# A hybrid decoder step: the prompt's last 16 tokens take gathered expert rows, and dense expert values come out with features in partitions

## The chip, the cores and the metric

The kernel runs on one core of one Trainium2 chip. The metric is the device time of one execution in microseconds (us), start to end. The program is written in a tile language whose scheduler sets the order of the instructions of each engine when the kernel is built; on the chip each engine then works through its own list in that order.

## The reference, cut to what matters

Two layers, each with a mixer (four kinds of heads side by side), a cross-attention and an expert part. 256 prompt tokens and 8 sample tokens go through them together, 264 columns in all. The change concerns the expert part. For every token and each of 8 heads it picks 16 of 16384 experts from 128 x 128 keys; an expert is a row of `u` and a row of `v`, 1024 numbers each:

```python
top_s, pick = lax.top_k(cand, PEER_TOPK)
e = jnp.take_along_axis(cidx, pick, axis=-1)
g = jax.nn.softmax(top_s, axis=-1)
act = jax.nn.gelu(jnp.einsum('td,thkd->thk', hb, u_tab[e]).astype(jnp.float32))
return jnp.einsum('thk,thkd->td', (g * act).astype(hb.dtype), v_tab[e])
```

So a token needs 128 rows of u, a gelu, a weight for each, and the weighted sum of 128 rows of v.

## The kernel before, in words

**Two ways to do the experts.** The 256 prompt tokens are done densely: all 16384 rows of u are multiplied with all 256 tokens, and a token's weight is zero for an expert that it did not pick. The 8 sample tokens are done sparsely: their 128 rows are gathered by index. The function is `peer`, from line 1585 on.

**Dense u** (`u_tile`, line 1638). Experts come in 128 tiles of 128. A tile of u (128x1024, 512 KB) is loaded by SP into one of three buffers `w`, split into a high part `wh` (ScalarE, line 313) and a low part `wl` (VectorE, line 298), and multiplied with the normed tokens, split likewise into `hh` and `hl` (`proj`, line 342): 8 pieces of the features times 3 products are 24 matmuls of 256 columns, called mm in the trace. ScalarE takes the gelu into HG0 (first 64 tiles) or HG1. `mm`, the helper, records every matmul at line 288. In the order's rows, names after the arrow are the two operands.

**Choosing and gating.** While the first 64 tiles run, VectorE and TensorE choose the experts of the prompt in two halves of 128 tokens, then of the sample tokens (lines 1651 to 1702). Then 64 gating steps (loop over `t4`, line 1745) make for 4 tokens each a 128x128 matrix of weights out of two one-hot matrices `ga` and `gb` (8 f16 matmuls into g), multiply it into HG, and compute one more tile of u.

**Sample rows.** In every fourth gating step one sample token gets its turn: for the first 32 steps `sample_u` (line 1708), then `sample_v`. `sample_u` gathers 128 rows of u (`us`, by the index tile `gi`) through GpSimd's queue into one of the three `w` buffers, SP broadcasts the token (`hd`, in DRAM) into `hb`, one buffer of 128x1024, and VectorE multiplies and sums them in one instruction (line 307) into `ac` (`sac`); three small instructions make its column of `wz`. `sample_v` gathers the rows of v and adds them up by 4 narrow matmuls, called sv, into `os_`.

**Dense values** (loop over `i2`, line 1773). A tile of v is loaded and split as u is, and HG is split into `ghl`. The output has tokens in partitions: 4 accumulators `acc` (pv in the trace) of 128 tokens x 512 features, 12 matmuls of 512 columns a tile. At the end `total` (line 1801) copies each accumulator, transposes it in four matmuls, adds it to the residual `x`, which has features in partitions, and squares it for the next norm.

**What sets the order.** The scheduler, from its own estimates of when an instruction can start. Hand-set places are the sv matmuls (kept together, given priority) and the last pv matmuls with the transposes.

Of the kernel before, what the change touches and what calls it, by code (L numbers as in the profile page):

```python
# [230 lines left out]
NF = 4  # L231
XT = 12
GS = 16384.0
# [10 lines left out]
def emit(tc, A, O, layers=(0, 1)):  # L244
# [305 lines left out]
    def rwkv(l, bp_, mp, cm, vc, inp, pre, st_rs, ymix):  # L550
# [85 lines left out]
        def unit(c, n0, zz=None):  # L636
# [69 lines left out]
            for i in range(1, 6):  # L706
# [3 lines left out]
                xl = tl([128], "xl", "xl")  # L710
# [874 lines left out]
    def peer(l, vc, xo, oo, xe, following):  # L1585
# [23 lines left out]
        hd = pe.enter_context(tc.tile_pool(name="d%d" % l, bufs=1, space=MemoryType.DRAM)).tile([8, 1024], F32, name="hd")  # L1609
        gi = fp.tile([128, 2, 8], I32, name="gi")  # L1610
        gs = fp.tile([128, 8], F32, name="gs")
# [5 lines left out]
        for c in range(16):  # L1617
            if c == 4:
                rms(tp, vc('norm_ffn'), r, hf, (hh, hl))
                for j in range(2):  # L1620
                    o = ps([8, 512], "h8")
                    for k in range(4):
                        T.transpose(o[:, k * 128:k * 128 + 128], hf[:, 4 * j + k, 256:264], ident)
                    h8 = tp.tile([8, 512], F32, name="h8", tag="sk")
                    S.copy(h8, o)
                    nc.sync.dma_start(hd[:, j * 512:j * 512 + 512], h8)
# [7 lines left out]
        HG0 = h0p.tile([128, 64, 256], F32, name="HG0")  # L1634
# [3 lines left out]
        def u_tile(i2, t0=0):  # L1638


            o = proj(A['ud'][l, i2], (hh[:, :, 0:256], hl[:, :, 0:256]), 256)
            d = HG0[:, i2, :] if i2 < 64 else HG1[:, i2 - 64, :]
            if t0:
                a = fp.tile([128, 256], F32, name="ua", bufs=2)
                act(a[:, 0:t0], o[:, 0:t0], AF.Gelu_apprx_tanh)
                tt(d[:, 0:t0], d[:, 0:t0], a[:, 0:t0], OP.mult)
            if t0 < 256:
                act(d[:, t0:256], o[:, t0:256], AF.Gelu_apprx_tanh)

        cur_tag[0] = "ps"  # L1650
        for i in range(2):
# [22 lines left out]
            tt(el[:, 1, ti], wt[:, 0, ti], wt[:, 1, ti], OP.subtract)  # L1674

# [25 lines left out]
        ts(gi, o[:, 0:2, :], float(l * 16384), op0=OP.add)  # L1701
        V.tensor_copy(gs, o[:, 2, :])
# [17 lines left out]
        def sample_v(b):  # L1720
            v = wp.tile([128, 1024], F32, name="w", tag="w", bufs=3)
            nc.gpsimd.indirect_dma_start(out=v, out_offset=None, in_=A['vd'].rearrange("l a b d -> (l a b) d"),
                                         in_offset=bass.IndirectOffsetOnAxis(ap=gi[:, 1, b:b + 1], axis=0))

            with together():
                for j in range(4):
                    mm(os_[j * 32:j * 32 + 32], wz[:, b, :], v[:, j * 256:j * 256 + 256], start=b == 0, stop=b == 7, skip=True)

        def sample_out():
# [5 lines left out]
            d = x[:, :, 256:264].rearrange("p (j c) b -> p c j b", c=2)  # L1735
            tt(d, d, o.rearrange("p c (j q) -> p c j q", j=4)[:, :, :, 0:8], OP.add)
# [4 lines left out]
            [128, 64, 256], F32, name="HG1")  # L1741
        ac = fp.tile([128, 4, 8], F32, name="sac")
        wz = fp.tile([128, 8, 32], F32, name="wz")
        os_ = ps([128, 256], "sv", "pr")
        for t4 in range(64):
# [124 lines left out]
```

## Time and profile before

| | |
|---|---|
| median of 3 runs | 2450.73 us (2449.32 to 2453.59) |
| profiled execution | 2446.82 us |
| its span, first to last instruction | 2445.1 us |
| TensorE busy | 2374.8 us, 97% |
| VectorE busy | 1749.7 us, 72% |
| ScalarE busy | 1378.9 us, 56% |
| moved by DMA | 480.63 MB |

The profile is one execution. Busy time is a union: two overlapping instructions of one engine count once. Matmuls overlap, so a matmul's own length says little of what it costs; the distance between two starts does. In layer 0 the choosing of experts runs from about 447 to 603 us, the gating to 852, the values from 858 to 1220; in layer 1 the expert part ends with the kernel. "PEclk" is the granted clock of TensorE as a share of 2.4 GHz.

### The profile page before, as it was taken

The page shows a single profiled execution, that of the slowest core. Times are in us where ns is not written, and L with a number is a line of the kernel's source. Part 1 is how long each engine was busy: PE and PEld are TensorE (multiplying, and loading weights), DVE is VectorE, ACT ScalarE, POOL GpSimd, SP SyncE. Part 2 cuts the span into 40 slices and gives each one's busy share as a digit, 9 for nine tenths or more (in the row PEclk, how much of TensorE's full clock was granted, in tenths as well). Part 3 has the DMA queues.
Part 4 walks back from the last instruction along what each step waited for, and adds up shares of the span by engine and source line. Part 5 has one row for each costly group of instructions (what it writes and reads, how often), then busy time and mean ns, then how long its engine had stood idle before and what let it go on. Part 6 is the DMA issues. An engine that isn't in the chain of part 4 may idle for free.

```text
span 2445.1 us, 46669 instructions
## 1 busy us (share of the span) xinstructions
PE 2374.8 (97%) x17292; PEld 2123.9 (87%) x17292; DVE 1749.7 (72%) x3875; ACT 1378.9 (56%) x2826; POOL 267.6 (11%) x288
## 2 busy tenths in 40 slices
PE   9898999999999999999998989999999999999998
PEld 7776979999999988878787779899999999888886
DVE  6757767997698855565568567689967987555555
ACT  5445565554687744544554456655547876444444
POOL 5741000000000000000057400000000000000000
PEclk9999999999999999999999999999999999999999
DMA  8733775555675555565577428755556755566554
GB/s 286 231 110 113 268 300 201 174 179 174 205 235 186 191 178 189 193 208 187 188 230 226 125 95 311 273 191 174 178 181 214 232 182 184 185 189 188 187 188 137
DMA packets 146372, 480.63 MB, mean 197 GB/s; under 512 B 20288, under 2 KB 37728, under 8 KB 141024
## 3 DMA queue, kind: packets, MB, share of 16 engines
q1 hardware_dynamic: 129088, 423.46, 52.8%
q0 software_dynamic: 17056, 54.17, 7.4%
q8 instruction: 137, 2.24, 0.4%
q14 instruction: 91, 0.75, 0.1%
HBM read 468.53 MB, written 9.03 MB: 195 GB/s over the span
## 4 chain that ended last, share of the span: by engine, by line
PE 88%; DMA 5%; ACT 2%; DVE 2%; issue 1%; SPq 1%; POOL 1%; DVEq 0%; ACTq 0%; POOLq 0%
PE mm L288 43%; PE pv L288 29%; PE g L288 3%; PE mv L288 2%; DMA kvp<-in_kc 2%; PE asc L288 1%; PE mk L288 1%; DMA kvp<-in_vc,vidx 1%; PE xo L288 1%; PE xm L288 1%; PE sc L288 1%; PE xl L288 1%; PE xp L288 1%; PE apv L288 1%; DVE wl L298 1%
## 5 line engine op out<-in xcount | busy, mean ns | idle before, releaser
L313 ACT CAST wh<-w 128x1024 fp32r<-128x1024 f32 x662 | 694.3, 1050 | 756.8 <-PE pv L288 358.4
L298 DVE TENSOR_TENSOR wl<-w,wh 128x1024 fp32r<-128x1024 f32 x662 | 807.3, 1221 | 432.5 <-ACT wh L313 427.8
L288 PE MATMUL mm<-hh,wh 128*128 128x256 f32 (+1 forms) x2176 | 545.9, 288 | 3.7 <-ACT HG L310 2.9
L288 PE MATMUL mm<-hl,wh 128*128 128x256 f32 (+1 forms) x2176 | 536.2, 284 | 0.0
L288 PE MATMUL pv<-wh,ghl 128*128 128x512 f32 x2048 | 524.5, 396 | 0.4 <-ACT ghl L313 0.4
L288 PEld LDWEIGHTS pv<-wh,ghl 128*128 128x128 f32 x2048 | 385.1, 188 | 92.8 <-ACT ghl L313 0.9
L288 PEld LDWEIGHTS mm<-hh,wh 128*128 128x128 f32 x2176 | 410.3, 189 | 5.6 <-ACT HG L310 4.0
L288 PEld LDWEIGHTS mm<-hl,wh 128*128 128x128 f32 x2176 | 410.2, 189 | 3.3 <-issue 3.3
L288 PE MATMUL mm<-hh,wl 128*128 128x256 f32 (+1 forms) x2176 | 300.5, 281 | 0.0
L288 PE MATMUL pv<-wl,ghl 128*128 128x512 f32 x1024 | 283.6, 396 | 0.0
L288 PEld LDWEIGHTS mm<-hh,wl 128*128 128x128 f32 x2176 | 276.3, 188 | 0.4 <-issue 0.4
L288 PEld LDWEIGHTS pv<-wl,ghl 128*128 128x128 f32 x1024 | 192.4, 188 | 46.5 <-DVE wl L298 0.8
L310 ACT ACTIVATE gb<-ga,ewt 128x128 f16<-128x128 f16 x512 | 173.1, 433 | 19.8 <-DVE ga L298 16.2
L1226 POOL DMA_INDIRECT kvp<-in_kc,pidx x128 | 144.9, 1132 | 234.6 <-ACT eh L310 179.0
L288 PE MATMUL mm<-eh,wh 128*128 128x264 f32 x624 | 162.0, 294 | 0.0
L288 PE MATMUL mm<-el,wh 128*128 128x264 f32 x624 | 160.5, 290 | 0.0
L288 PEld LDWEIGHTS mm<-eh,wh 128*128 128x128 f32 x624 | 117.9, 189 | 4.9 <-issue 3.7
L288 PEld LDWEIGHTS mm<-el,wh 128*128 128x128 f32 x624 | 118.1, 189 | 3.0 <-issue 2.1
L298 DVE TENSOR_TENSOR ghl<-HG,ghl 128x256 fp32r<-128x256 f32 x256 | 106.7, 417 | 0.0
L313 ACT CAST ghl<-HG 128x256 fp32r<-128x256 f32 x256 | 101.8, 398 | 2.4 <-DVE HG L298 2.4
L298 DVE TENSOR_TENSOR HG<-HG,g 128x256 f32<-128x256 f32 (+31 forms) x254 | 86.2, 347 | 16.7 <-PE g L288 15.9
L1710 POOL DMA_INDIRECT w<-in_us,gi x16 | 16.8, 1053 | 713.3 <-DVE wl L298 418.9
(674 smaller groups left out, 3304.6 us busy)
## 6 DMA issues: line engine op xcount, KB each, us to landing
w<-in_ud SPq DMA_DIRECT2D x256, 512.0 KB
w<-in_vd SPq DMA_DIRECT2D x256, 512.0 KB
w<-in_w_in SPq DMA_DIRECT2D x46, 512.0 KB
kvp<-in_kc SPq DMA_DIRECT2D x128, 128.0 KB
xkt<-in_mk SPq DMA_DIRECT2D x16, 1024.0 KB
xkt<-in_mv SPq DMA_DIRECT2D x16, 1024.0 KB
w<-in_peer_wq SPq DMA_DIRECT2D x32, 512.0 KB
w<-in_x_wk SPq DMA_DIRECT2D x16, 512.0 KB
```

The costliest lines, as they stand in the source:

```text
L288: T.matmul(out, lhsT, rhs, start=start, stop=stop, skip_group_check=skip)
L298: (eng or V).tensor_tensor(out, a, b, op=op)
L310: S.activation(out, a, f, **kw)
L313: S.copy(h, x)
L1226: nc.gpsimd.indirect_dma_start(out=t[:, j, :], out_offset=None, in_=A['kc'].rearrange("l n p f -> (l n p) f"), in_offset=bass.IndirectOffs ...
L1710: nc.gpsimd.indirect_dma_start(out=u, out_offset=None, in_=A['us'], in_offset=bass.IndirectOffsetOnAxis(ap=gi[:, 0, b:b + 1], axis=0))
```

## The change

The last 16 prompt tokens (`NS`) join the 8 sample tokens: 24 rows (`NR`) are gathered, and 240 tokens (`ND`) are dense. So every dense matmul of u has 240 columns, there are 60 gating steps, and four tiles of u follow the last step. The indices of the 16 tokens are read out of the second half's choice (`ne`, into `gi`).

The gathers have two buffers of their own (`eg`) and no longer take one of the three for weights. All 24 rows of u come before all 24 rows of v, spread evenly over the 60 steps; gelu and weights for all are made once between them (`rows_gate`), and `wz` is zeroed once by GpSimd.

In the dense values the operands change sides: the tile of v is the stationary one, HG the moving one. The result has features in partitions, 8 pieces of 240 columns in 4 accumulators; each takes 3 matmuls a tile, 24 in all. `total` and its transposes are gone: VectorE adds each piece from PSUM to `x`, ScalarE squares it.

One more line, in the RWKV part of the mixer, lets the second group's copies `xl` use buffers of their own.

```diff
-                xl = tl([128], "xl", "xl")
+                xl = tl([128], "xl", "xm" if n0 else "xl")
...
-            o = proj(A['ud'][l, i2], (hh[:, :, 0:256], hl[:, :, 0:256]), 256)
+            o = proj(A['ud'][l, i2], (hh[:, :, 0:ND], hl[:, :, 0:ND]), ND)
...
-        def sample_u(b):
-            u = wp.tile([128, 1024], F32, name="w", tag="w", bufs=3)
-            nc.gpsimd.indirect_dma_start(out=u, out_offset=None, in_=A['us'],
-                                         in_offset=bass.IndirectOffsetOnAxis(ap=gi[:, 0, b:b + 1], axis=0))
+        def gather(src, k, b):
+            e = fp.tile([128, 1024], F32, name="eg", bufs=2)
+            nc.gpsimd.indirect_dma_start(out=e, out_offset=None, in_=src,
+                                         in_offset=bass.IndirectOffsetOnAxis(ap=gi[:, k, b:b + 1], axis=0))
+            return e
+
+        def row_u(b):
+            u = gather(A['us'], 0, b)
             hb = fp.tile([128, 1024], F32, name="hb")
             nc.sync.dma_start(hb, bc(hd[b:b + 1], 128, 1024))
-            c = slice(b, b + 1)
-            stt(u, u, 1.0, hb, OP.mult, OP.mult, accum_out=ac[:, 0, c])
-            act(ac[:, 2, c], ac[:, 0, c], AF.Gelu_apprx_tanh)
-            tt(ac[:, 3, c], ac[:, 2, c], gs[:, c], OP.mult)
-            ts(wz[:, b], cg['iota'][:, 0:32], float(b), ac[:, 3, c], OP.is_equal, OP.mult)
+            stt(u, u, 1.0, hb, OP.mult, OP.mult, accum_out=ac[:, 0, b:b + 1])
+
+        def rows_gate():
+
+            act(ac[:, 1], ac[:, 0], AF.Gelu_apprx_tanh)
+            wf = wz.rearrange("p a b -> p (a b)")[:, 0:NR * 33].rearrange("p (a b) -> p a b", b=33)
+            tt(wf[:, :, 0], ac[:, 1], gs, OP.mult)
...
-        for t4 in range(64):
+        steps = ND // 4
+        for t4 in range(steps):
...
-            if t4 % 4 == 3:
-                (sample_u if t4 < 32 else sample_v)(t4 // 4 % 8)
-        sample_out()
+            r0, r1 = (2 * NR * k // steps for k in (t4, t4 + 1))
+            for r in range(r0, r1):
+                if r == NR:
+                    rows_gate()
+                row_u(r) if r < NR else row_v(r - NR)
+        rows_out()
+        for i in range(64 + steps, 128):
+            u_tile(i, ND)
...
-        acc = [ps([128, 512], "pv%d" % i, ("pa", "pr")[i // 2]) for i in range(4)]
+        acc = [ps([128, 2, ND], "pv%d" % i, ("pa", "pr")[i // 2]) for i in range(4)]
...
-                m, d = slice((i % 2) * 128, (i % 2) * 128 + 128), slice((i // 2) * 512, (i // 2) * 512 + 512)
-                for k, (a, b) in enumerate(((gh, vh), (gh, vl), (gl, vh))):
-                    mm(acc[i], a[:, m], b[:, d], start=i2 + n == 0 and k == 0, stop=i2 + n == 127 and k == 2)
+                d = slice(c * 128, c * 128 + 128)
+                for k, (a, b) in enumerate(((vh, gh), (vl, gh), (vh, gl))):
+                    mm(acc[c // 2][:, c % 2, :], a[:, d], b, start=i2 + n == 0 and k == 0 and c % 2 == 0,
+                       stop=i2 + n == 127 and k == 2, skip=True)
...
+                        d = x[:, c, 0:ND]
+                        stt(d, acc[c // 2][:, c % 2, :], 1.0 / GS, d, OP.mult, OP.add)
```

Where the instructions stand now, at three places of layer 0.

On SP, in the gating steps, the queue that loads weight tiles (w) and broadcasts the tokens of the rows (hb). Before:

```order
L1713 DMA hb<-hd 128x1024
L332 DMA w<-in_ud 128x1024 x4
L1713 DMA hb<-hd 128x1024
L332 DMA w<-in_ud 128x1024 x4
L1713 DMA hb<-hd 128x1024
```

After:

```order
L336 DMA w<-in_ud 128x1024 x2
L1729 DMA hb<-hd 128x1024
L336 DMA w<-in_ud 128x1024 x3
L1729 DMA hb<-hd 128x1024
L336 DMA w<-in_ud 128x1024 x2
L1729 DMA hb<-hd 128x1024
```

A broadcast stood behind every fourth weight tile and stands behind every second now.

On VectorE, in the gating steps, between two reductions of a gathered row, after the change (before, 26 such rows lie between two, with 4 of wl):

```order
L311 SCALAR_TENSOR_TENSOR eg,sac<-eg,hb 128x1024
L302 TENSOR_TENSOR HG_5778<-HG_5778,g 128x64x4
L302 TENSOR_TENSOR HG_8349<-HG_8349,g 128x12x4
L302 TENSOR_TENSOR ga<-iota_5205,et 128x1024
L302 TENSOR_TENSOR wl<-w,wh 128x1024
L302 TENSOR_TENSOR HG_8349<-HG_8349,ua 128x52
L302 TENSOR_TENSOR gb<-ga,etl 128x2x256
L302 TENSOR_TENSOR HG_5778<-HG_5778,g 128x64x4
L302 TENSOR_TENSOR HG_8349<-HG_8349,g 128x13x4
L302 TENSOR_TENSOR ga<-iota_5205,et 128x1024
L302 TENSOR_TENSOR wl<-w,wh 128x1024
L311 SCALAR_TENSOR_TENSOR eg,sac<-eg,hb 128x1024
```

Two weight tiles and about two gating steps lie between two reductions now; the first rows come even ahead of the first gating step.

On TensorE, the end of the layer (pv: values; tp: transposes of ov, the copy of an accumulator; var: sums for the norm). Before:

```order
L1806 MATMUL tp<-cst_g,ov 128x128 x4
L288 MATMUL pv_12007<-wh,ghl 128x512
L288 MATMUL pv_12007<-wl,ghl 128x512
L288 MATMUL pv_12007<-wh,ghl 128x512
L1806 MATMUL tp<-cst_g,ov 128x128 x4
L288 MATMUL pv_12009<-wh,ghl 128x512
L288 MATMUL pv_12009<-wl,ghl 128x512
L288 MATMUL pv_12009<-wh,ghl 128x512
L1806 MATMUL tp<-cst_g,ov 128x128 x4
L288 MATMUL var<-s_14785,cst_g 128x128 x4
```

After, inside the value part:

```order
L292 MATMUL pv_12134<-ghl,wh 128x240
L292 MATMUL pv_12134<-ghl,wl 128x240
L292 MATMUL pv_12134<-ghl,wh 128x240 x2
L292 MATMUL pv_12134<-ghl,wl 128x240
L292 MATMUL pv_12134<-ghl,wh 128x240
L292 MATMUL pv_12135<-ghl,wh 128x240
```

The transposes have left the list, and each accumulator takes two groups of three matmuls with 240 columns where it took one of three with 512.

## Rows read from the trace of the kernel before

**Rows 1.** The page: TensorE busy, and the chain that ended last.

```profile
PE 2374.8 (97%) x17292; PEld 2123.9 (87%) x17292; DVE 1749.7 (72%) x3875; ACT 1378.9 (56%) x2826; POOL 267.6 (11%) x288
PE mm L288 43%; PE pv L288 29%; PE g L288 3%; PE mv L288 2%; DMA kvp<-in_kc 2%; PE asc L288 1%; PE mk L288 1%; DMA kvp<-in_vc,vidx 1%; PE xo L288 1%; PE xm L288 1%; PE sc L288 1%; PE xl L288 1%; PE xp L288 1%; PE apv L288 1%; DVE wl L298 1%
```

**Rows 2.** Windows, layer 0: choosing experts, gating steps, expert values.

```profile
core 0: us, PE busy (x) PEld busy (x) DVE busy (x) ACT busy (x) POOL busy (x), PEclk, DMA share, GB/s
447.00:603.00 156.00, 153.92 (x1317) 152.60 (x1316) 145.28 (x474) 81.63 (x126) 0.00 (x0) 1.00 0.54 173
640.00:852.00 212.00, 212.00 (x2014) 204.41 (x2013) 187.32 (x400) 167.51 (x496) 15.21 (x15) 1.00 0.65 209
858.00:1214.00 356.00, 355.55 (x1532) 286.27 (x1531) 202.17 (x296) 173.33 (x260) 3.20 (x5) 1.00 0.60 190
```

**Rows 3.** TensorE timeline: start, length, line, tiles, shape, run of instructions.

```profile
619.85 1.11 PE L288 MATMUL mm<-hh,wl 128*128 128x256 f32 x8
1184.50 2.03 PE L288 MATMUL pv<-wh,ghl 128*128 128x512 f32 x8
700.90 0.63 PE L288 MATMUL g<-gb,ga 128*128 128x128 f16 x8
```

**Rows 4.** TensorE groups by shape: busy us, mean ns, idle before.

```profile
L288 PE MATMUL mm<-hh,wl 128*128 128x256 f32 x2048 | 282.3, 281 | 0.0
L288 PE MATMUL g<-gb,ga 128*128 128x128 f16 x1024 | 91.0, 221 | 0.0
L288 PE MATMUL mk<-mem,w 128*128 128x128 f32 x256 | 29.4, 276 | 2.2 <-DMA w<-in_x_wk 2.2
L288 PE MATMUL var<-s,cst_g 128*128 128x8 f32 x32 | 3.8, 246 | 0.0
L288 PE MATMUL sv<-w,wz 128*32 128x256 f32 x128 | 10.2, 391 | 0.0
```

**Rows 5.** VectorE groups in the gating steps, 640 to 852 us.

```profile
L298 DVE TENSOR_TENSOR wl<-w,wh 128x1024 fp32r<-128x1024 f32 x62 | 75.7, 1221 | 12.3 <-ACT wh L313 12.2
L298 DVE TENSOR_TENSOR ga<-iota,et 128x1024 f16<-128x1024 f16 x61 | 42.0, 689 | 0.0
L298 DVE TENSOR_TENSOR HG<-HG,g 128x256 f32<-128x256 f32 x123 | 41.4, 345 | 8.2 <-PE g L288 7.9
L298 DVE TENSOR_TENSOR gb<-ga,etl 128x512 f16<-128x512 f16 x61 | 25.4, 417 | 0.3
L298 DVE TENSOR_TENSOR HG<-HG,ua 128x4 f32<-128x4 f32 (+60 forms) x61 | 17.0, 279 | 0.0
L307 DVE SCALAR_TENSOR_TENSOR w<-w,hb 128x1024 f32<-128x1024 f32 x8 | 9.8, 1224 | 4.4 <-DMA w<-in_us,gi 4.3
```

**Rows 6.** Timeline of a sample row's reduction, the next broadcast, and line 1710's landings.

```profile
642.51 1.23 DVE L307 SCALAR_TENSOR_TENSOR w<-w,hb 128x1024 f32<-128x1024 f32 x1 [1.41 <-DMA w<-in_us,gi]
644.15 0.47 SPq L1713 DMA_DIRECT2D hb<-hd  x1
DMA to landing us min/median/max: 4.3/4.6/4.9
```

**Rows 7.** The window with the densest transfers, same columns as Rows 2.

```profile
1520.00:1540.00 20.00, 19.53 (x190) 16.60 (x189) 14.57 (x32) 15.01 (x35) 0.57 (x1) 1.00 1.01 405
```

**Rows 8.** Timeline of the end of the last layer.

```profile
2431.30 0.39 PE L288 MATMUL pv<-wh,ghl 128*128 128x512 f32 x1
2433.97 0.68 DVE L298 TENSOR_TENSOR x<-x,tp 128x512 f32<-128x512 f32 x1
2434.76 0.63 ACT L310 ACTIVATE s<-x 128x512 f32<-128x512 f32 x1 [1.02 <-DVE x L298]
2435.44 1.16 PE L288 MATMUL var<-s,cst_g 128*128 128x128 f32 x8 [0.19 <-ACT s L310]
2436.64 0.48 ACT L310 ACTIVATE rstd<-var,small 128x264 f32<-128x264 f32 x1 [1.25 <-PE var L288]
```

More of the change, by code (lines that the diff above doesn't have):

```diff
@@ L231 @@
 NF = 4
+NS = 16
+ND = SEQ - NS
+NR = NS + 8
 XT = 12
@@ L1674, in peer @@
             tt(el[:, 1, ti], wt[:, 0, ti], wt[:, 1, ti], OP.subtract)
+            if i:
+                V.tensor_copy(gs[:, 0:NS], o[:, 2, 128 - NS:128])
+                ge = tp.tile([128, 2, NS], F32, name="ge")
+                V.tensor_copy(ge, o[:, 0:2, 128 - NS:128])
+                ne = tp.tile([128, 2, NS], F32, name="ne")
+                for k in range(2):
+                    stt(ne[:, k], ge[:, k], 128.0, ge[:, 1 - k], OP.mult, OP.add)
+                ts(gi[:, :, 0:NS], ne, float(l * 16384), op0=OP.add)
         s16 = tp.tile([128, 1, 2, 16], F32, name="s16s")
@@ L1777, in peer, with terms @@
                 hs = HG0[:, i, :] if i < 64 else HG1[:, i - 64, :]
-                ghl = fp.tile([128, 2, 256], F32R, name="ghl", tag="ga", bufs=2)
+                ghl = fp.tile([128, 2, ND], F32R, name="ghl", tag="ga", bufs=2)
                 split(ghl[:, 0], ghl[:, 1], hs)
                 part.append((vh, vl, ghl[:, 0], ghl[:, 1]))
-            def terms(i, n):
+            def terms(c, n):
                 vh, vl, gh, gl = part[n]
-                m, d = slice((i % 2) * 128, (i % 2) * 128 + 128), slice((i // 2) * 512, (i // 2) * 512 + 512)
-                for k, (a, b) in enumerate(((gh, vh), (gh, vl), (gl, vh))):
-                    mm(acc[i], a[:, m], b[:, d], start=i2 + n == 0 and k == 0, stop=i2 + n == 127 and k == 2)
-            for n in range(2 if i2 < 126 else 1):
-                for i in range(4):
-                    terms(i, n)
+                d = slice(c * 128, c * 128 + 128)
+                for k, (a, b) in enumerate(((vh, gh), (vl, gh), (vh, gl))):
+                    mm(acc[c // 2][:, c % 2, :], a[:, d], b, start=i2 + n == 0 and k == 0 and c % 2 == 0,
+                       stop=i2 + n == 127 and k == 2, skip=True)
+            with (tc.manual_schedule(engines={mybir.EngineType.PE}) if i2 in (0, 126) else ExitStack()):
+                if i2 < 126:
+                    for n in range(2):
+                        for c in range(8):
+                            terms(c, n)
+                else:
+                    for c in range(8):
+                        for n in range(2):
+                            terms(c, n)
+                        d = x[:, c, 0:ND]
+                        stt(d, acc[c // 2][:, c % 2, :], 1.0 / GS, d, OP.mult, OP.add)
             if i2 == 62:
@@ L1793, in peer @@
                 v = ps([128, NT], "var", "ps")
-                s2 = fp.tile([128, 8, 8], F32, name="s2", tag="ua", bufs=2)
-                act(s2, x[:, :, 256:264], AF.Square)
+                s2 = fp.tile([128, 8, NR], F32, name="s2", tag="ua", bufs=2)
+                act(s2, x[:, :, ND:264], AF.Square)
                 act(warm, part[0][2][:, 0:1].bitcast(F32), AF.Sqrt, scale=0.0)
                 for c in range(8):
-                    mm(v[:, 256:264], cg['o1024'], s2[:, c, :], start=c == 0, stop=False, skip=True)
-        def total(i):
-            ov = fp.tile([128, 512], F32, name="ov", tag="gb", bufs=2)
-            act(ov, acc[i], AF.Copy, scale=1.0 / GS)
-            o = ps([128, 4, 128], "tp", "mm")
-            for c in range(4):
-                T.transpose(o[:, c, :], ov[:, c * 128:c * 128 + 128], ident)
-            n = slice((i % 2) * 128, (i % 2) * 128 + 128)
-            d = x[:, 4 * (i // 2):4 * (i // 2) + 4, n]
-            tt(d, d, o, OP.add)
-            s2 = fp.tile([128, 4, 128], F32, name="s2", tag="ga", bufs=2)
-            act(s2, d, AF.Square)
-            return s2, n
-        q = []
-        with tc.manual_schedule(engines={mybir.EngineType.PE}):
-            terms(0, 1)
-            for i, nx_ in ((0, 2), (2, 1), (1, 3), (3, None)):
-                if nx_ is not None:
-                    terms(nx_, 1)
-                q.append(total(i))
-        for i, (s2, n) in enumerate(q):
-            for c in range(4):
-                mm(v[:, n], cg['o1024'], s2[:, c, :], start=False, stop=i == 3 and c == 3, skip=True)
+                    mm(v[:, ND:264], cg['o1024'], s2[:, c, :], start=c == 0, stop=False, skip=True)
+        for c in range(8):
+            s2 = fp.tile([128, ND], F32, name="s2", tag="gb", bufs=2)
+            act(s2, x[:, c, 0:ND], AF.Square)
+            mm(v[:, 0:ND], cg['o1024'], s2, start=False, stop=c == 7, skip=True)
         cur_tag[0] = "pa"
```

46 lines of the change are left out of this document (23 added, 23 removed).

## The prediction

> **What bounds the kernel now.** I read the page first. TensorE is busy 97% of the span, and the chain that ended last goes through the matmuls called mm (43%) and pv (29%) [rows 1]. The mm are the first projection of the experts (u), and the pv the second (the values). So I went to the windows of the expert stage [rows 2]. While experts are chosen TensorE is busy 153.9 of 156 us, in the gating steps 212 of 212 and in the value part 355.6 of 356, all at a granted clock of 1.00, the 2.4 GHz level. VectorE stands at 93%, 88% and 57%, ScalarE at most at 79%, the DMA share at most at 0.65. TensorE sets the pace, then, and VectorE is the engine with the least room behind it, except in the value part. The second layer repeats this.
>
> What a matmul costs there is its distance from the one before, not its own length. From a run's length less the last one's own time: 256 columns (1.11 - 0.281) / 7 = 118.4 ns, 512 columns (2.03 - 0.39) / 7 = 234.3 ns, the gating's 128 columns of f16 (0.63 - 0.221) / 7 = 58.4 ns [rows 3, 4].
>
> **The change, part by part.** Sums are for both layers.
>
> *Pitch of a matmul with 240 columns.* No row has one. From 512 to 256 columns the pitch falls (234.3 - 118.4) / 256 = 0.453 ns a column, so 240 would take 118.4 - 7.2 = 111.2 ns. Below that something else may hold it. Each matmul loads 128x128 weights, and plain f32 records with 8 moving columns still take 3.8 us for 32, 119 ns each, and with 128 columns 29.4 us for 256, 115 ns each [rows 4]; some of that is the first one's start. If loads of the kind used here need as long, 240 columns gain next to nothing. So the bounds are 111.2 and 118.4 ns, no gain. I take 112, near the low end: the 256-column pitch still lies on a line with the 512-column one, hardly above 106.7 ns of streaming at 2.4 GHz, and shows no sign of a floor yet.
>
> The Trainium skill (TensorE: Matmul & The Clock Gate, LDWEIGHTS) gives a load of 128 columns about 107 ns. By that the floor lies under 111.2, the pitch is 111.2, and the sum below would be 10 us better; the f32 rows, at 115 to 119 ns, stand above its figure.
>
> *Dense u.* 128 tiles of 24 matmuls in two layers are 6144; 240 columns instead of 256 save 6.4 ns each: -39.3 us. Bounds 0 and -44.
>
> *Dense values.* Before: 128 tiles of 12 matmuls with 512 columns, 3072 x 234.3 = 719.8 us. After: features are the partitions, so 24 matmuls with 240 columns, 6144 x 112 = 688.1 us. -31.7 us, bounds -36 and +8. The work per column is a sixteenth less, but the number of matmuls doubles, so the small fixed part of each is paid twice.
>
> *Gating.* 60 steps instead of 64 drop 4 x 8 f16 matmuls a layer: 64 x 58.4 ns = -3.7 us.
>
> *Gathered rows on TensorE.* 16 sample rows (8 a layer) cost 10.2 us of sv [rows 4], 0.64 us each; 32 more are +20.4 us. Nothing hides them, since TensorE has no gaps. Bounds +15 and +25.
>
> *Gathered rows on VectorE.* A row of u is a 128x1024 reduction of 1.224 us [rows 5]; there are 24 instead of 8 a layer. The three small instructions per row become one set for all, and the gating multiplications lose 4 steps. In the gating steps VectorE's recorded times add up to more than its busy time, since neighbours overlap (212 and 187 us, a factor of 0.87). By the order, the rows of u now come one for two weight tiles. Where gating runs, some 15 rows a layer, one row goes with two tiles and 1.9 steps. VectorE then has 2 x 1.221 for wl, 1.9 x 2.06 for gating ((42.0 + 41.4 + 25.4 + 17.0) / 61) and 1.31 for the row and its read: 7.7 us recorded, 6.7 at 0.87. TensorE has 48 x 0.112 + 15 x 0.0584 = 6.25 us. VectorE becomes the later one by 0.43 us a row, times 30 rows: +13 us. Bounds: 0, if leftover u tiles even it out, and +39, if each of the 32 new reductions stands on the path in full. I stay in the lower half because the rows of v, in the second half of the steps, leave VectorE alone.
>
> *Transfers.* A row of u needs a gather and a broadcast of hd into hb, 0.52 MB each; with two weight tiles that is 2.1 MB in 6.25 us, 336 GB/s. A stretch of before moved 405 GB/s [rows 7], so bandwidth alone fits. The chain per row is the tighter thing. hb is one buffer: its load is issued 0.4 us after the reduction that frees it [rows 6], and lands, if it takes as long as the gathers, 4.6 us later; with 1.23 us of reduction that is 6.2 to 6.3 us per row against 6.25 to 6.7 available. I count 0 here. Its bounds are 0 and the rival below. What waits behind a late hb is the whole of VectorE's queue, wl of the next weight tile first, and then TensorE. On SP a broadcast waiting for its buffer holds back the weight loads behind it. The gathers no longer take one of the three weight buffers, which helps a little; I count that as 0 too.
>
> *End of a layer.* The last pv ends at 2431.69 us, and the root starts at 2436.64, 4.95 us later: copy, four transposes, addition 0.68, squares 0.63, eight sums 1.16 [rows 8]. After: one addition of 240 columns from PSUM and its squares (about 0.4 each, from 0.68 and 0.63 at 512) and one sum, with the hops some 2 us. That is -3 us, and as much in the first layer; with the transposes that stand between the last pv groups and go too, -7 us, bounds -12 and 0.
>
> *The rest* (24 rows of hd instead of 8, index sums for 16 tokens, a zeroed wz on GpSimd, another buffer for one copy in the RWKV part) is a few instructions of 0.15 to 0.4 us beside a busy TensorE: 0, or some 3 us either way through a shifted order.
>
> Sum: -39.3 - 31.7 - 3.7 + 20.4 + 13 + 0 - 7 = -48 us. The profiled execution took 2446.8 us (span 2445.1 and 1.7 around it), so 2398.5; the median of the runs is 3.9 us above the profiled one, which gives **2402 us**.
>
> **Rivals.**
>
> *Everything hides.* VectorE's rows find cover and the pitch is 111.2: -44 - 36 - 3.7 + 20.4 - 7 = -70, 2381 us. For it: 12% of VectorE was idle in the gating steps. Against: its load per step goes up just where rows of u run.
>
> *A slow row chain.* Each row of u takes 6.7 to 7.5 us because hb lands late behind two weight loads. 48 rows x 0.4 to 1.3 us: 2420 to 2450, 2430 in the middle. For it: one buffer, and transfers rise from 209 GB/s [rows 2] to 336. Against: the gathers landed evenly, 4.3 to 4.9 us, with a quarter of the rows [rows 6].
>
> *The row chain gives the gain away* (slower). The same chain, at 8 us a row: 48 x 1.75 = 84 less the 13 already counted, 2473 us. It decides from about 7.5 us a row on. Against: that needs a broadcast landing some 6 us after its issue.
>
> *A weight-load floor* (slower). The pitch stays at 118.4 however few the columns. Then u saves 0 and the values cost +7.6; with -3.7 + 20.4 - 7, and VectorE hidden again, +17: 2468 us. Break-even is 115.9 ns. For it: the f32 rows at 115 to 119 ns. Against: the straight line to 256.
>
> *Many matmuls cost more than columns do* (slower): the value part pays per matmul, so twice the number takes longer. By rows, a fixed part is 118.4 - 256 x 0.453 = 2.4 ns, 24 of them 0.06 us a tile, already in the sum. The Trainium skill (TensorE: Matmul & The Clock Gate, Back-to-back issue gap) states sustained pitches of 131 ns at 512 columns and 81 at 128. By that rule a value tile goes from 12 x 131 to 24 x 96 ns, and the estimate is +185 us. The trace disagrees at 512, with 234.3 ns, so I give it one chance in a hundred.
>
> That the change doesn't do what it says is excluded: the new order has 240-column matmuls and 24 rows.
>
> **How the numbers follow.** Forecast 0.43 (own range 2390 to 2420), all hidden 0.20, slow chain 0.20, chain that gives the gain away 0.07, floor 0.06, many matmuls 0.01, and 0.03 for no change by shifted orders elsewhere. About 0.2%, 5 us, is what a measurement tells from no change. A tenth of the slow chain's cases ends that close to before: faster 0.81, same 0.05, slower 0.14. The range runs from 2374, a little under all hidden, to 2446, most of the slow chain.
>
> **What would show it.** Right: u runs at 111 to 113 ns a matmul, a value part of about 342 us a layer instead of 360, sv near 31 us, VectorE above 93% where rows of u run with TensorE gaps of a few us. Wrong: pitches near 118 ns, long waits of VectorE's reduction for hd or us, weight loads waited for by ScalarE in that stretch, or gains that come from somewhere else, such as the mixers.

## The result, and the profile after

The changed kernel takes **2469.0 us** in the median (2465.7 to 2473.2), the kernel before 2450.1 on the same chip: ratio 1.0075, with an interval of 1.0059 to 1.0092. It is 0.75% slower, where 2% faster was forecast, and lies above the range (2374 to 2446).

The page of the changed kernel, the rows that answer to [rows 1]:

```profile
PE 2347.4 (95%) x20492; PEld 2207.6 (90%) x20492; DVE 1761.4 (71%) x3895; ACT 1360.5 (55%) x2764; POOL 347.8 (14%) x354
PE pv L292 28%; PE mm L292 25%; DMA hb<-hd 9%; DMA eg<-in_vd,gi 4%; DMA kvp<-in_kc 2%; DVE wl L302 2%; PE mv L292 2%; PE asc L292 1%; PE mk L292 1%; DVE eg L311 1%; PE xo L292 1%; PE xl L292 1%; ACT wh L317 1%; PE z L292 1%; PE sc L292 1%
```

TensorE is busy 27 us less, and the execution is longer. The chain that ended last now goes through the broadcasts of hd (9%) and the gathers of v (4%), and mm has fallen from 43% to 25% of it. Windows of layer 0, as [rows 2]: choosing, rows of u, rows of v, values.

```profile
441.00:577.00 136.00, 134.00 (x1203) 132.32 (x1202) 132.94 (x436) 72.60 (x114) 0.00 (x0) 1.00 0.58 179
577.00:749.00 172.00, 152.98 (x1364) 147.22 (x1363) 132.06 (x275) 106.81 (x270) 31.78 (x25) 0.97 0.85 289
749.00:847.00 98.00, 89.84 (x894) 75.99 (x894) 68.62 (x143) 61.98 (x186) 25.76 (x23) 0.98 0.75 246
882.00:1238.00 356.00, 352.51 (x3100) 350.76 (x3099) 206.99 (x311) 178.33 (x275) 6.04 (x9) 1.00 0.66 195
```

The second and third rows are the place. TensorE is without work for 19.0 and 8.2 us, where it had no gap in the gating steps before [rows 2], and the granted clock is 0.97 and 0.98 in them, a mean of its levels of 2.4 and 1.2 GHz. VectorE is *less* busy than before (132 of 172 us), so it is not short of time; it waits. VectorE's group of the row products, and TensorE's of the value rows, in layer 0 (busy, mean ns, idle before them and what ended it):

```profile
L311 DVE SCALAR_TENSOR_TENSOR eg<-eg,hb 128x1024 f32<-128x1024 f32 x24 | 29.4, 1224 | 32.9 <-DMA hb<-hd 30.0 <-DMA eg<-in_us,gi 2.9
```

```profile
L292 PE MATMUL sv<-eg,wz 128*32 128x256 f32 x192 | 15.2, 393 | 8.0 <-DMA eg<-in_vd,gi 7.9
```

The products cost what they did [rows 5], 1.224 us, but VectorE stood 32.9 us in front of 24 of them, 30.0 of it for the broadcast. What TensorE, in turn, waited for between 560 and 880 us, the three longest (us in total, times, longest):

```profile
PE sv L292 <- DMA eg<-in_vd,gi: 7.9, 8, 2.3
PE g L292 <- DVE gb L302: 7.2, 7, 2.6
PE mm L292 <- DVE wl L302: 3.5, 6, 0.8
```

The second and third are instructions that stand behind the products in VectorE's list. How a row goes, in the chain of waits between 604 and 628 us (start, length, what):

```profile
604.05 0.23 DVE eg L311
...
605.31 5.80 DMA hb<-hd
...
611.20 0.12 DVE eg L311
...
612.46 5.68 DMA hb<-hd
...
618.24 1.25 DVE eg L311 x2
...
619.50 7.33 DMA hb<-hd
...
626.92 0.12 DVE eg L311
```

Product, broadcast, product, with nothing between: the one buffer hb is free when a product ends, the next broadcast is issued 0.03 us later and lands 5.7 to 7.3 us after that, and VectorE waits for it. Over all 18 products of the u rows that waited for it, the broadcast landed 4.6 to 7.8 us after its issue, 6.0 in the median. A row of u takes 7.2 us (21 rows from 598 to 749 us).

By the two profiled executions the spans differ by 2463.7 - 2445.1 = +18.6 us. Placed by the start of the first matmul with the normed tokens (hh), the start of the first pv, the end of the last pv and the start of the norm's root:

| both layers, us | forecast | measured |
|---|---|---|
| expert stage up to the values: 441.7 and 441.1 before, 471.5 and 465.9 after | -9.6 | +54.6 |
| values, first to last pv: 362.7 and 361.5, 356.1 and 353.1 | -31.7 | -15.0 |
| end of the layers: 7.2 and 4.9, 5.1 and 1.6 | -7 | -5.4 |
| everything else | 0 | -15.6 |

The first row's forecast is -39.3 for u, -3.7 for the gating, +20.4 for sv and +13 for VectorE. The pitch came out as forecast: eight matmuls of 240 columns take 1.06 us, so (1.06 - 0.280) / 7 = 111.4 ns, by the reckoning of [rows 3].

```profile
880.74 1.06 PE L292 MATMUL mm<-hh,wl 128*128 128x240 f32 x8
```

The end of the last layer, which answers to [rows 8]: the last pv, one addition, its square, two sums and the root, 1.9 us from the first row's start to the last's.

```profile
2452.74 0.28 PE L292 MATMUL pv<-ghl,wh 128*128 128x240 f32 x1
2453.05 0.41 DVE L311 SCALAR_TENSOR_TENSOR x<-pv,x 128x240 f32<-128x240 f32 x1 [0.77 <-PE pv L292]
2453.49 0.40 ACT L314 ACTIVATE s<-x 128x240 f32<-128x240 f32 x1 [1.11 <-DVE x L311]
2453.95 0.67 PE L292 MATMUL var<-s,cst_g 128*128 128x240 f32 x2 [0.53 <-ACT s L314]
2454.66 0.48 ACT L314 ACTIVATE rstd<-var,small 128x264 f32<-128x264 f32 x1 [0.76 <-PE var L292]
```

### The profile page after: what moved, and what is told of

The parts are those of the page before. It is cut to its first block, busy times and chain, and to the rows that moved or that the text cites. A ratio compares the mean times of both kernels' runs of the same rounds, so it can differ in the third digit from the quotient of the medians.

```text
span 2463.7 us, 53212 instructions
## 1 busy us (share of the span) xinstructions
PE 2347.4 (95%) x20492; PEld 2207.6 (90%) x20492; DVE 1761.4 (71%) x3895; ACT 1360.5 (55%) x2764; POOL 347.8 (14%) x354
## 4 chain that ended last, share of the span: by engine, by line
PE 68%; DMA 18%; DVE 6%; issue 4%; ACT 2%; POOL 1%; SPq 1%; DVEq 0%; POOLq 0%; ACTq 0%
PE pv L292 28%; PE mm L292 25%; DMA hb<-hd 9%; DMA eg<-in_vd,gi 4%; DMA kvp<-in_kc 2%; DVE wl L302 2%; PE mv L292 2%; PE asc L292 1%; PE mk L292 1%; DVE eg L311 1%; PE xo L292 1%; PE xl L292 1%; ACT wh L317 1%; PE z L292 1%; PE sc L292 1%
## 5 line engine op out<-in xcount | busy, mean ns | idle before, releaser
L292 PE MATMUL pv<-ghl,wh 128*128 128x240 f32 x4096 | 624.6, 275 | 3.2 <-ACT ghl L317 2.1
L292 PEld LDWEIGHTS pv<-ghl,wh 128*128 128x128 f32 x4096 | 562.5, 190 | 4.7 <-ACT ghl L317 2.4
L292 PE MATMUL mm<-hh,wh 128*128 128x240 f32 (+1 forms) x2176 | 524.6, 283 | 12.0 <-ACT HG L314 8.5
L292 PE MATMUL mm<-hl,wh 128*128 128x240 f32 (+1 forms) x2176 | 515.4, 278 | 0.0
L292 PE MATMUL pv<-ghl,wl 128*128 128x240 f32 x2048 | 445.1, 276 | 2.4 <-DVE wl L302 2.4
L292 PEld LDWEIGHTS pv<-ghl,wl 128*128 128x128 f32 x2048 | 331.9, 190 | 3.1 <-DVE wl L302 3.0
L292 PE MATMUL mm<-hh,wl 128*128 128x240 f32 (+1 forms) x2176 | 302.0, 280 | 6.2 <-DVE wl L302 6.0
L292 PE MATMUL g<-gb,ga 128*128 128x128 f16 x960 | 88.1, 222 | 17.2 <-DVE gb L302 10.8
L302 DVE TENSOR_TENSOR ghl<-HG,ghl 128x240 fp32r<-128x240 f32 x256 | 102.4, 401 | 0.3
L317 ACT CAST ghl<-HG 128x240 fp32r<-128x240 f32 x256 | 98.8, 387 | 4.2 <-DVE HG L302 3.1
```

What stands on the lines that cost most here:

```text
L292: T.matmul(out, lhsT, rhs, start=start, stop=stop, skip_group_check=skip)
L302: (eng or V).tensor_tensor(out, a, b, op=op)
L317: S.copy(h, x)
```

## Experiments

The kernel before took 2444.8 to 2464.2 us in the median on the chips used, so each kernel is given as its ratio to the runs of before on its own chip. Theories in the expectations: A, a row's chain through its few buffers; B, the products are too much for VectorE; C, too many bytes for the 16 DMA engines; D, the order packs the rows too densely. "Stage" is from the first matmul with hh to the first pv, layer 0 / layer 1; "product" and "sv" are the idle times in front of the row products on VectorE and of the value rows on TensorE in layer 0; "lead" is the median time from a broadcast's issue to the moment when its product's turn on VectorE has come (its start less its wait). The changed kernel itself stands there twice, on two chips, 1.0075 and 1.0050; smaller differences than between these two say little.

| kernel | ratio, 95% interval | stage, us | product, us | lead, us | sv, us |
|---|---|---|---|---|---|
| before | 1 | 441.7 / 441.1 | 4.4 (8 rows) | 11.7 | 0 |
| changed | 1.0075, 1.0059 to 1.0092 | 471.5 / 465.9 | 32.9 | 5.0 | 8.0 |
| changed, again | 1.0050, 1.0033 to 1.0068 | 469.6 / 462.7 | 27.9 | 5.1 | 8.6 |
| hb1load | 1.0004, 0.9986 to 1.0022 | 457.0 / 465.6 | 20.0 | | 4.4 |
| hb2 | 1.0022, 1.0001 to 1.0044 | 459.4 / 458.3 | 6.3 | 9.2 | 4.0 |
| ring3 | 1.0128, 1.0091 to 1.0165 | 469.6 / 472.3 | 22.5 | 5.1 | 5.8 |
| ns8 | 1.0004, 0.9987 to 1.0022 | 446.8 / 448.8 | 19.3 (16 rows) | 4.8 | 3.0 |
| sp16 | 0.9952, 0.9935 to 0.9969 | 451.0 / 450.2 | 8.1 | 7.0 | 6.1 |
| ring4sp16 | 0.9920, 0.9896 to 0.9944 | 446.9 / 446.5 | 7.4 | 7.2 | 0 |
| ring4sp16b | 0.9926, 0.9910 to 0.9942 | 451.5 / 445.7 | 8.3 | 7.6 | 0 |
| sp1 | 1.0099, 1.0083 to 1.0116 | 468.4 / 466.0 | 23.9 | 4.6 | 8.6 |
| poolq | 1.0083, 1.0061 to 1.0105 | 462.7 / 472.6 | 23.6 | 4.7 | 6.9 |
| u1gather | 1.0102, 1.0069 to 1.0135 | 463.6 / 465.3 | 31.3 | 3.7 | 6.5 |
| ring4 | 0.9921, 0.9899 to 0.9944 | 447.7 / 449.0 | 7.4 | 9.2 | 0 |
| memonly | 1.0061, 1.0039 to 1.0082 | 462.1 / 468.8 | 26.9 | 5.0 | 6.2 |
| sp8one | 0.9985, 0.9970 to 1.0000 | 444.5 / 445.8 | 21.9 (16 rows) | 4.3 | 0 |
| spread_halfhb | 0.9998, 0.9987 to 1.0009 | 457.9 / 457.8 | 42.9 | 3.0 | 0 |
| late_quarter | 0.9808, 0.9789 to 0.9827 | 432.8 / 435.1 | 2.4 | 9.2 | 0 |
| late_full | 0.9884, 0.9863 to 0.9906 | 440.8 / 443.6 | 3.1 | 8.2 | 0 |
| pvonly | 0.9980, 0.9962 to 0.9998 | 440.5 / 439.9 | 5.1 (8 rows) | 11.8 | 0 |

### First: four ways to ease the row

```diff
 hb1load:  one broadcast a layer, all rows use it
-            hb = fp.tile([128, 1024], F32, name="hb")
-            nc.sync.dma_start(hb, bc(hd[b:b + 1], 128, 1024))
+            if b == 0: hbs.append(...); nc.sync.dma_start(hbs[0], ...)
 hb2:      two buffers
+            hb = fp.tile([128, 1024], F32, name="hb", bufs=2)
 ring3:    broadcasts and gathers share three buffers
+            hb = fp.tile([128, 1024], F32, name="hb", tag="eg", bufs=3)
 ns8:      eight gathered prompt tokens
-NS = 16
+NS = 8
```

hb2 and all kernels below with more buffers find their memory in a helper of the gating weights, which keeps half of what it kept. Expected of hb1load: 

> Leaves out 23 of the 24 broadcasts of a token into hb in each layer: all 24 rows of u are multiplied with the first row's token; gathers and reductions stay. Theory A (the chain through the one hb buffer, reduction, issue, landing, next reduction, sets the pace of the row stretch): VectorE's 54.9 us of waiting for hb go, and the kernel comes to about 2430 us. Theory B (the 128x1024 reductions are too much for VectorE): nothing changes, 2469 us within 5. Theory C (the 16 DMA engines are full, 0.85 of their time at 289 GB/s): a quarter of the stretch's bytes goes, about 2440 us.

Of hb2: 

> Two hb buffers instead of one, so a broadcast is under way while the row before is reduced; the same bytes. The 4 KB for it come from two helper halves of the gating weights that are kept no longer than they are read. Theory A: about 2435 us. Theory B: 2469 within 5. Theory C: the bytes are the same, at most 10 us better, 2459 or more.

Of ring3: 

> The two gather buffers and hb become one ring of three, so the rows of v have three buffers in place of two; the rows of u see the same order of waits as before. Theory A with the same chain in the v rows (a buffer comes free only after the sv matmuls, and a gather lands 7 us after its issue): TensorE's 36 us of waiting for v rows shrink to about 10 and the clock holds, about 2450 us. Theories B and C: no change beyond 5 us.

Of ns8: 

> 8 prompt tokens instead of 16 take gathered rows: 248 dense columns, 62 steps, 16 rows of u over about the same stretch, so three weight tiles lie between two rows in place of two. Theory A: the chain of 7.2 us a row fits beside 9 us of TensorE, its waits go, and 15.2 instead of 30.7 us of sv remain; with a pitch of 115 ns about 2420 us. Theory B: still 2/3 of the added reductions, about 2455 us. Theory C: 1.6 MB less per three tiles, the engines at about 0.75, about 2425 us.

None came near the time of theory A. hb1load and ring3 fit no theory; ns8 took the time of B (2455; 1.0004 of 2450 is 2451, within 5), and hb2 came within 4 us of the least that C allowed (2459; 1.0022 is 2456). Without the broadcasts VectorE waits for the gathers, which have two buffers, instead:

```profile
L311 DVE SCALAR_TENSOR_TENSOR eg<-eg,hb 128x1024 f32<-128x1024 f32 x24 | 29.3, 1223 | 20.0 <-DMA eg<-in_us,gi 20.0
```

A row of u needs two of ring3's three buffers, so the next row can't be under way in full: no cure, and slower. ns8 waits nearly as long for each row (1.2 us, 1.4 in the changed kernel) in fewer rows. B gets no support: no kernel with waits gone and the same products stays at 1.0075.

hb2 is a limit of all that follows. Its lead is 9.2 us and its products wait 6.3 us, none of it for a broadcast, and yet it gained only 0.3 to 0.5%. What TensorE waited for most there, between 560 and 880 us, is the high part of a weight tile, from ScalarE:

```profile
PE mm L292 <- ACT wh L317: 8.1, 9, 1.4
PE sv L292 <- DMA eg<-in_vd,gi: 4.0, 6, 1.2
```

Why wh was late there was not tried.

### Order or buffers

In hb2 the rows of u stand one in 5 us and then the stage has 77 us without rows, which brought up D. The spread order puts them wide apart:

```diff
 sp16 (with hb2), ring4sp16 (with the ring of four), sp1 (alone): order
+        due = [52 + 2.1 * k for k in range(NR)] + [103 + 1.0 * k for k in range(NR)]
+            with tc.issue_after(tile_w[int(due[b])]):
                 nc.sync.dma_start(hb, bc(hd[b:b + 1], 128, 1024))
+            with tc.issue_after(tile_mm[int(due[NR + b])]), together():
 ring4, ring4sp16: ring of four
+            hb = fp.tile([128, 1024], F32, name="hb", tag="eg", bufs=4)
+            e = fp.tile([128, 1024], F32, name="eg", tag="eg", bufs=4)
```

sp16: 

> The changed kernel with two hb buffers and an order of its own for the row steps: each broadcast of hd is placed behind the weight load of expert tile 52 + 2.1 b, and each value row's matmuls behind the matmuls of tile 103 + b, so the 48 row steps are spread over tiles 52 to 126 instead of standing close together and leaving 100 us of the stage without rows. All bytes are the same. A, the chain through one hb buffer: as with two buffers alone, 2464. B, too much for VectorE: 2469. C, too many bytes for the 16 engines over the whole stage (78.6 MB in 238 us, 330 GB/s): not under 2460, since no byte goes. D, it is the dense packing that starves the weight loads for a stretch: the stage from the first q matmul to the first pv matmul falls from 470 to about 445 us a layer, so 2469 - 2 x 22 = 2425, and the DMA share stays under 0.85 in every stretch of it.

ring4sp16: 

> The same spread order, with the broadcasts and the value gathers in one ring of four buffers, so that a value row's gather may be issued up to four rows ahead (with two buffers it landed 6.8 to 7.9 us after its issue and TensorE waited 36 us for value rows in both layers). A: under the spread order alone by the value rows' waits, 2410 to 2430. C: not under 2460. D: 2420 to 2430, like the spread order alone, since rows that stand apart leave a gather time to land with two buffers too.

The changed kernel again: 

> The changed kernel itself once more, beside the spread kernels on one chip, as the mark for their ratios: 1.0075 as before, 2475 if the kernel before takes 2457.

ring4sp16b, the same kernel as ring4sp16: 

> The ring of four with the spread order once more, on the same chip as the changed kernel: ratio 0.992 again, so 1.5% under the changed kernel. If the lead came from the chip of the day and not from the order, it shrinks to under 0.5%.

sp1: 

> The spread order alone: one hb buffer and two gather buffers as in the changed kernel. The u rows stand one in 2.1 tiles, some 7.0 us, which is what the chain through one hb buffer takes (7.2 us a row), so SP and VectorE should still wait for the broadcast there; only the value rows are freed. Theory A (chain and queue, buffers and order are both needed): stage 460 a layer, ratio 1.002 to 1.005. Theory D (the order alone is the cause): as with two buffers, ratio 0.995.

ring4: 

> The ring of four buffers for broadcasts and value gathers in the changed kernel's own dense order. If buffers and order are both needed: as with two hb buffers alone, 1.000 to 1.003. If four buffers are enough without the order: 0.993.

memonly: 

> The changed kernel with the gating weights' helper alone in half the memory, as all kernels with more buffers have it; buffers and order as in the changed kernel. If the helper has no part: ratio 1.005 to 1.0075 as the changed kernel; if it has, under 1.002.

Spread and buffers together made the kernel faster than before, and again on another chip (0.9920, 0.9926). The order alone did not: sp1, at 1.0099, came out above both values expected of it and slower than the changed kernel on the same chip (1.0050). And then the ring of four in the *dense* order did as much as in the spread one (0.9921), as expected if four buffers are enough. So D falls: the order adds something to two buffers (1.0022 to 0.9952) and nothing to four. C falls too, as ring4 moves all the bytes, and more densely. Its window of the u rows:

```profile
577.00:749.00 172.00, 161.53 (x1521) 151.19 (x1520) 147.86 (x321) 114.25 (x291) 42.30 (x38) 0.99 0.93 338
```

TensorE is busy 161.5 us there instead of 153.0, at a DMA share of 0.93 and 338 GB/s. The helper has no part (memonly, 1.0061).

### Which queue

```diff
 poolq:
-            nc.sync.dma_start(hb, bc(hd[b:b + 1], 128, 1024))
+            nc.gpsimd.dma_start(hb, bc(hd[b:b + 1], 128, 1024))
 u1gather:
-            u = gather(A['us'], 0, b)
+            if b == 0: us0.append(gather(A['us'], 0, b))
+            u = us0[0]
-            stt(u, u, 1.0, hb, ...)
+            stt(hb, u, 1.0, hb, ...)
```

poolq: 

> The changed kernel with one edit: the broadcasts of hd are issued by GpSimd instead of SyncE, so a broadcast that waits for the one hb buffer no longer stands ahead of weight loads in SyncE's queue (28.7 + 17.4 us of such waits in layer 0). Order and buffers stay. Theory A1, SyncE's queue is what starves the weights: TensorE's idle time in the row stages falls from 26 to under 10 us a layer, ratio 0.998. Theory A2, VectorE's own queue is it (the row's product waits for the broadcast ahead of the splits of weights, 30 us in layer 0): the waits stay, ratio 1.006 to 1.008. Theory C: no byte goes, ratio 1.0075.

u1gather: 

> The changed kernel with the gather of expert u rows done once a layer: every row step multiplies the same gathered rows, so 46 gathers of 0.52 MB (24 MB in all) are left out, while all broadcasts of hd, sums and value rows stay. A, the chain through hb: the broadcast alone still takes 5 to 7 us, so little changes, 2465. B: 2469. C and D, bytes: 24 MB at 340 GB/s is 70 us of 16 engines, so the waits for weights in the u rows go and the stage is shorter by 10 to 15 us a layer, 2440 to 2450.

In the changed kernel a broadcast that waits for its buffer stands ahead of weight loads in SP's queue:

```profile
SPq L1729 <- DMA hb<-hd: 28.7, 16, 4.3
SPq L1729 <- DVE eg L311: 17.4, 13, 1.8
```

The Trainium skill (DMA: Bandwidth & Descriptors, Anatomy of one DMA — SWDGE (gpsimd) path) says that a DMA waits for semaphores on the engine that issues it, before it is sent; the two rows show that here. But to take them away gained nothing: with the broadcasts issued by GpSimd these waits are gone from SP, VectorE's stay (23.6 us), and the time too (1.0083). Nor did 24 MB fewer gathers help (u1gather, 1.0102; its one gathered tile also holds one of the two gather buffers through the u rows, and its product is written over hb). What is left is VectorE's own queue.

### The product's place in VectorE's queue

The first kernel (spread_halfhb) was meant for the bytes: it loads a quarter of each broadcast and leaves three quarters of each dot product out. It became slower than ring4sp16, and the scheduler had put the product nearer to its smaller broadcast: the lead fell from 7.2 to 3.0 us. The second, late_quarter, asks for one thing, the product two weight splits later. The lists of SP and GpSimd are the same in both; but on VectorE the split changed its place too, and stands right behind gb in 104 cases, both layers together, instead of 40, where it mostly stood right behind ga.

```diff
 spread_halfhb (on ring4sp16):
-                nc.sync.dma_start(hb, bc(hd[b:b + 1], 128, 1024))
-            stt(u, u, 1.0, hb, OP.mult, OP.mult, accum_out=ac[:, 0, b:b + 1])
+                nc.sync.dma_start(hb[:, 0:256], bc(hd[b:b + 1, 0:256], 128, 256))
+            stt(u[:, 0:256], u[:, 0:256], 1.0, hb[:, 0:256], ...)
 late_quarter (on spread_halfhb), late_full (on ring4sp16):
+            with tc.issue_after(tile_wl[int(due[b])]):
                 stt(...)
```

spread_halfhb: 

> The ring of four with the spread order, and of each broadcast only a quarter (256 of the 1024 columns; the row's product and sum run over these alone, so three quarters of each dot product are left out). 24 x 0.39 MB = 9.4 MB a layer go, of 78.6 after the choosing, and VectorE has some 0.8 us a row less. If bytes are what still costs there (16 engines' share 0.90 in the u rows), the idle 6 to 8 us of TensorE in the u rows go and the stage is 5 to 10 us a layer shorter: ratio 0.985 to 0.988. If not, 0.992.

late_quarter: 

> The spread kernel with a quarter of each broadcast (256 of 1024 columns; three quarters of each dot product left out), with one edit: each u row's product stands two weight splits later in VectorE's queue (one later than with whole broadcasts), so that the broadcast has landed when the product's turn comes. Bytes, buffers and SyncE's queue stay. If VectorE's wait for the broadcast, with splits queued behind it, is what costs TensorE the time: VectorE's waits on the broadcast fall from 40 us to under 10 in layer 0, TensorE's idle time in the u rows from 16 us to under 8, ratio 0.990. If it is something else (the form of the smaller broadcast, the bytes), 1.000.

late_full: 

> The ring of four with the spread order and whole broadcasts, with each u row's product one weight split later in VectorE's queue. VectorE waits only 4.5 us there, so little is left to gain: 0.992, and not under 0.989 (idle time of TensorE in the u rows from 7 us to 4 us a layer). Were it slower by 0.3% or more, the longer hold of the buffers would be felt.

spread_halfhb, VectorE's group of products in layer 0:

```profile
L313 DVE SCALAR_TENSOR_TENSOR eg<-eg,hb 128x256 f32<-128x256 f32 x24 | 10.2, 424 | 42.9 <-DMA hb<-hd 40.6 <-DMA eg<-in_us,gi 2.3
```

Its window of the u rows:

```profile
577.00:749.00 172.00, 157.78 (x1446) 151.50 (x1445) 124.64 (x311) 111.44 (x292) 25.48 (x24) 0.99 0.76 240
```

And what TensorE waited for in that window (us in total, times, longest):

```profile
PEld mm L294 <- DVE wl L304: 11.5, 14, 1.8
PE mm L294 <- DVE wl L304: 8.6, 13, 1.6
```

late_quarter, the same group and the same window:

```profile
L313 DVE SCALAR_TENSOR_TENSOR eg<-eg,hb 128x256 f32<-128x256 f32 x24 | 10.1, 419 | 2.4 <-DMA eg<-in_us,gi 2.4
```

```profile
577.00:749.00 172.00, 171.22 (x1658) 168.99 (x1657) 147.78 (x358) 130.17 (x345) 28.54 (x28) 1.00 0.84 276
```

TensorE's waits in spread_halfhb are the link: it waits for wl, the split that stands behind the waiting product. In late_quarter no such wait is left. With the product's turn 9.2 us after its broadcast's issue instead of 3.0, the wait is gone, TensorE is busy 171.2 of 172 us, and the ratio goes from 0.9998 to 0.9808. Same bytes, same buffers, same SP queue. The gain was expected at 1% (0.990) and came out twice as large; how much of it is the product's place and how much the split's was not taken apart. With whole broadcasts the same kind of edit moves the product one split later, and there the split stands behind gb about as often as in ring4sp16 (52 cases, 48): the products wait 3.1 us instead of 7.4 to 8.3, and the ratio goes from 0.9920 and 0.9926 to 0.9884 (0.9863 to 0.9906), just below what I had set as the lower end. That is the lowest ratio of a kernel that computes all of it, **2415.9 us against 2444.9** for the kernel before on that chip. Its group of products, and its window:

```profile
L313 DVE SCALAR_TENSOR_TENSOR eg<-eg,hb 128x1024 f32<-128x1024 f32 x24 | 29.3, 1219 | 3.1 <-DMA eg<-in_us,gi 2.9 <-DMA hb<-hd 0.2
```

```profile
577.00:749.00 172.00, 168.03 (x1586) 163.71 (x1585) 157.24 (x343) 125.59 (x322) 31.00 (x28) 1.00 0.90 322
```

### Two parts alone

```diff
 sp8one: NS = 8, one hb buffer, order
+        due = [50 + 3.1 * k for k in range(NR)] + [101 + 1.6 * k for k in range(NR)]
 pvonly: the kernel before, with the values of the changed kernel at 256 columns
```

sp8one: 

> Eight gathered prompt tokens in place of 16 (so 16 row steps a layer and 248 dense columns), one hb buffer, and an order that gives each u row 3.1 tiles, some 10.5 us, and each value row 1.6 tiles, 5 us. The chain through one buffer takes 7 us a row. If a row's room against its chain is what decides, TensorE's idle time falls to under 6 us a layer although there is only one buffer, and the stage is its work of 426.6 us and some 10 more: 437 to 440 a layer, ratio 0.993 (the same eight tokens in dense order: 1.0004). If several buffers are needed whatever the order, 1.000.

pvonly: 

> The kernel before with the value part alone changed: the dense expert values are computed with features in partitions, at all 256 columns; every row stays where it was. By the pitches (two matmuls of 256 columns at 118.4 ns for one of 512 at 234.3) the values cost 2 x 1536 x (236.8 - 234.3) = +7.6 us, and the end of the layers gives 7 back: 2457 against 2457 for the kernel before on this chip, ratio 1.000. If the part has a gain or a cost beyond the pitch (the values measured 10 to 14 us a layer shorter in the changed kernel, where the pitch alone asks for 16), it shows here: ratio 0.995 or 1.004.

sp8one missed the 0.993 that room alone would have given, and came nearer to the other value, 1.000: a row had some 10 us for a chain of 7, and VectorE still waited 21.9 us in 16 rows. The table says why: room for the chain isn't a lead. The product's turn came 4.3 us after the issue, and the broadcast (5.7 us to landing in the median) was not there. pvonly shows that the new form of the values is no loss by itself, 0.998 (0.9962 to 0.9998); 128 tiles of 24 matmuls took 364.6 and 358.3 us a layer against 362.7 and 361.5 of before.

## Why the prediction was wrong

- **Transfers: "I count 0 here."** This is the step that failed. It set the broadcast's landing at 4.6 us, from gathers [rows 6] in a kernel with 16 gathered rows in 64 steps, where now there are 48 in 60, and so got 6.2 to 6.3 us a row, just inside the room. The broadcasts landed 6.0 us after issue in the median, beside weight loads and gathers at a DMA share of 0.85, and 4.6 was the shortest of 18; with 1.23 us of product a row takes 7.2 us. The step named what waits behind a late hb ("the whole of VectorE's queue, wl of the next weight tile first, and then TensorE"), and the experiments on the product's place bear that out; but it priced it at nothing, because with 4.6 us the chain just fitted. In the u rows of the first layer alone TensorE was without work for 19.0 us.
- **The two rivals of the row chain.** By its pace, 7.2 us a row, the kernel is "a slow row chain" (6.7 to 7.5, 2420 to 2450, chance 0.20). By its time, 2469, it is "the row chain gives the gain away" (8 us a row, 2473, chance 0.07). So both had the mechanism, and the second its time partly by luck: by the prediction's own formula 7.2 us a row are 48 x 0.95 = 46, less 13, and 2435. The other 34 us are terms that came out worse, the value rows, whose gathers no part of the sum let TensorE wait for (8.0 us in each layer), another 15 in the stage that were not taken apart (a part of them at the lower clock), the values (17) and the ends (2), less 16 of everything else. "A slow row chain" has 2420 as its lower end without the 13 that its upper end takes off; with them it is 2408.
- **Dense values, -31.7: measured -15.0.** The pitch in runs is as forecast, but the mean distance over all 3072 pv of a layer is 115.9 and 114.9 ns, against 236.1 and 235.2 for 1536 before. Much of the difference lies in few places: ten and nine pairs of pv stand over 0.3 us apart, and these hold 8.6 and 6.7 us beyond the pitch (before, 4.2 and 2.9). Seven pairs in each layer lie in the last 11 us, where additions to x and the norm's sums now come between the last pv. So a part of what the layers' ends gave is paid here. A term by pitch leaves such stops out.
- **VectorE rows, +13.** In the changed kernel VectorE was not the later engine, it was 77% busy there. Without the waits it may become so: late_full and late_quarter differ by 8 us a layer, and they differ in 9.4 MB a layer, in 0.8 us of product a row and in the split's place alike. Which of these it is was not tried.
- **Dense u, gating, sv, end of a layer.** The pitch of 111.4 ns is as forecast, so the weight-load floor was wrong, and so was "many matmuls". (The floor's break-even of 115.9 ns counts the 13 us of VectorE that its sum leaves out; without them it is 117.0.) By the Trainium skill's figures (TensorE: Matmul & The Clock Gate, Back-to-back issue gap) 240 columns would go at some 96 ns, an estimate; the trace has 111.4. The value rows cost 15.2 us of matmuls a layer, 0.63 each, as forecast; the layers' ends gave 5.4 of 7.
- **The rest, 0: measured -15.6** between the two profiled executions, 10.1 of it between the norm's root at the end of layer 0 and the first matmul with hh of layer 1, the mixer and the cross-attention (401.3 us before, 391.2 after). The line for `xl` did not shorten that stretch on another chip, where it took 401.3 us both without the line (pvonly) and with it (sp16); with the line it took 389.5 to 405.0 us over all profiles. The line alone was not run, so what shortened the mixers stays open.

Even late_full needs 440.8 and 443.6 us for the stage, as long as before (441.7 and 441.1). Its gain over the kernel before is that of the values, the ends and the mixers; the narrower u pays for the rows, no more.

## What to carry to other kernels

A load that fits by bandwidth may still be late at one instruction, and in an in-order queue everything behind that instruction is late with it. Count, for each load, the time from its issue to the turn of its first reader, and compare it with the landing time under the load of the *new* kernel, not the old; where it is short, move the reader a place or two later or give the load another buffer. Fewer bytes, another engine to issue from, or rows spaced apart gained little or nothing here as long as that lead was under the landing time. A lead alone is not enough either: hb2 had one of 9.2 us, and TensorE then waited for something else.

## What the runs showed of the hardware

- A quarter of the bytes did not land in a quarter of the time. By the few landings that the profile can place, 128 KB took 4.8 us in the median (spread_halfhb) and 4.3 (late_quarter), 512 KB took 6.6 (late_full and ring4), each beside weight loads. The 512 KB gathers that GpSimd issues took 4.6 us before [rows 6] and 7.4 in the u rows of the changed kernel. The Trainium skill (DMA: Bandwidth & Descriptors, Anatomy of one DMA — SWDGE (gpsimd) path) has some 2 us plus the bytes at 436 GB/s for a DMA that GpSimd issues, which would be an estimate of 3.2 us for 512 KB; under this load the trace has more than twice that.
- At a DMA share of 0.93 and 338 GB/s (ring4, u rows) TensorE was busy 161.5 us of 172, at 0.85 and 289 GB/s (the changed kernel) 153.0: the fuller DMA engines went with the busier TensorE.
- Beside gaps the clock may fall: in the changed kernel's u rows, with 19.0 us without work, the granted clock was 0.97 in the mean. From 717 to 729 us TensorE worked 7.9 of 12 us at 1.00, the 2.4 GHz level, and from 729 to 741 us the mean was 0.72, part of it at 1.2 GHz. In late_quarter, with 0.8 us without work, it was 1.00.
